# A transformer layer on one core: the second feed-forward product as seven products of block sums

## The chip, the core and the metric

The kernel runs on one core of a Trainium2 chip. The core has a matrix engine (TensorE, "PE" in the profile, with its weight loads as "PEld"), a vector engine (VectorE, "DVE"), a scalar engine (ScalarE, "ACT"), GpSimd ("POOL", hardly used here) and a queue that issues the transfers (SyncE, "SP"). Matrix results go to eight PSUM banks of 128 x 512 fp32; operands lie in SBUF.

The metric is the time of one execution on the device in microseconds (us). Before the change it is 2343.2 us, the median of 3 runs (2342.2 to 2344.59).

## What is computed

One layer for 512 tokens of width 2048, all in fp32: a modulated norm, two mixers, an output projection, a second modulated norm and a gated feed-forward part. The change concerns the last lines:

```python
h = rms_norm(x, norm2_g[layer]) * (1.0 + sc2) + sh2
gate, up = jnp.split(h @ w_ffn_in[layer], 2, axis=-1)
x = x + g2 * ((jax.nn.silu(gate) * up) @ w_ffn_out[layer])
```

The hidden width is 5632, that is 44 tiles of 128. The product with `w_ffn_in` is called the first product here, that with `w_ffn_out` the second.

## The kernel before

**Layout.** Activations lie feature by feature: a tile has 128 features on the partitions and the tokens (T = 512) along the free axis. Output feature tile m (16 of them) is thus a 128 x 512 matrix.

**Precision.** An fp32 matrix product is made of three fast ones. `split` (L208) makes of a weight tile a rounded high part (ScalarE, L212) and the rest (VectorE, L213). `three` (L219) multiplies high by high, high by low and low by high into one accumulator. The pools `hi` and `lo` have three buffers each, so `split` can run two tiles ahead of the one in use. Splits have a raised priority (`AHEAD`), by which the program that orders each engine's queue places them earlier than their place in the code.

**First product (L1015 to L1047).** For each f from 2 to 43 it is already made by seven products for eight: weights and activations are cut into blocks (two halves of k, gate and up for the weights; two token halves, HT = 256, for the activations), sums of blocks are made on VectorE (L1022 to L1025), and `product` (L898) runs 24 matmuls of 256 columns for each of the seven. Results are taken from PSUM by `tap` (L993, ScalarE). At the end `keep` (L1000) multiplies the gate by up, splits the 512 columns into a high and a low part and writes both to DRAM (`actd`, 512 KB for each f). While f is below 18, one task of `rest` per f also makes one column of the modulation vector from a 128 x 2048 matrix (`ada`, L185, and `gemv`, L178, on VectorE).

**Second product (L1051 to L1087).** The 44 tiles of hidden features are taken in chunks of 8, 12, 12 and 12, since all of them don't fit into SBUF. For each chunk and each m the weights `w_fo[m]` are loaded and split, and for each hidden tile `three` multiplies: the weights are stationary, the 512 tokens move. The accumulated 128 x 512 result is multiplied by the gate column and added to `x2[m]` by one fused operation on VectorE (L1083), and after the last chunk written to the output (L1085). Activations of the next chunk come in meanwhile (`load_acts`, L1055). That is 44 x 16 x 3 = 2112 matmuls of 512 columns.

**Order.** Each engine has a queue of its own, executed in order; the order in it was worked out ahead of time from priorities and readiness. All loads and stores are on SyncE's queue.

## Time and profile before

| what | us |
|---|---|
| median of 3 runs | 2343.2 (2342.2 to 2344.59) |
| the profiled execution | 2343.62 |
| its span, first to last instruction | 2341.8 |
| all work ahead of f = 2 of the first product | 0 to 1009.76 |
| first product, f = 2 to 43 | 1009.76 to 1859.30 |
| second product | 1859.30 to 2338.10 |
| what follows the last matmul | 2338.10 to 2341.8 |

In the first of these stages TensorE is busy for 975.62 us. Matmuls are pipelined, so the duration of one matmul in a row (0.389 us for 512 columns) is longer than the distance from one to the next; times for TensorE are read from distances between starts, or from the length of a piece over its count. The same holds, in a smaller way, for VectorE.

### The profile page before, as it was taken

Reading aid. Unit: us, or ns where it says so; the run is one execution under the profiler, and the core shown is the slowest. Engines: PE = TensorE matmul, PEld = TensorE weight load, DVE = VectorE, ACT = ScalarE, POOL = GpSimd, SP = SyncE. Lnnn points to the kernel's source line nnn. Section 1 sums busy time; section 2 is a strip of 40 time slices with the busy share of each in tenths; the row PEclk is TensorE's granted clock in tenths of the full one; section 3 lists DMA queues with packets and bytes.
Section 4 is the critical chain, followed back from the end, with each engine's and each line's share of the span. In section 5 each row is a group of like instructions: output and inputs, shape, how many; then the busy total and the mean of one; then the engine's idle time right before and its main releaser. Section 6 shows DMA issues by size and latency. Waiting matters only on the chain.

```text
span 2341.8 us, 35224 instructions
## 1 busy us (share of the span) xinstructions
PE 2303.9 (98%) x14371; PEld 2106.8 (90%) x14371; DVE 1646.8 (70%) x2208; ACT 1027.8 (44%) x1833; POOL 10.7 (0%) x25
## 2 busy tenths in 40 slices
PE   8999899999999999989999999999999999999999
PEld 6899899888888788989999999999999988888887
DVE  8887778998887864898888877777777633333332
ACT  4325665566556422744444444444444321222221
POOL 0000000000000000000000000000000000000000
PEclk9999999999999999999999999999999999999999
DMA  9886446843322575335544433333333584253331
GB/s 371 314 309 220 168 148 246 300 155 108 111 106 73 186 285 185 131 140 189 184 177 174 168 127 135 136 135 136 135 136 123 209 324 146 95 202 95 105 136 61
DMA packets 77549, 402.99 MB, mean 172 GB/s; under 512 B 8622, under 2 KB 9292, under 8 KB 47564
## 3 DMA queue, kind: packets, MB, share of 16 engines
q1 hardware_dynamic: 77388, 400.75, 47.4%
q8 instruction: 112, 1.84, 0.3%
q14 instruction: 49, 0.40, 0.0%
HBM read 369.24 MB, written 31.47 MB: 171 GB/s over the span
## 4 chain that ended last, share of the span: by engine, by line
PE 90%; DVE 6%; ACT 2%; issue 1%; DMA 1%; SPq 0%; ACTq 0%; DVEq 0%
PE ffA L92 21%; PE fo L92 20%; PE ffC L92 10%; PE sbp L92 7%; PE wo L92 7%; PE ffB L92 5%; PE st L92 4%; PE hgf L92 4%; PE hgq L92 3%; PE hgg L92 3%; PE l L92 1%; PE sbo L92 1%; DVE ada L178 1%; PE hgo L92 1%; PE r L92 0%
## 5 line engine op out<-in xcount | busy, mean ns | idle before, releaser
L92 PE MATMUL fo<-act,wfo_0h 128*128 128x512 f32 x1024 | 315.2, 389 | 0.0
L178 DVE SCALAR_TENSOR_TENSOR ada<-ada,cond 128x2048 f32<-128x2048 f32 x95 | 216.5, 2284 | 37.1 <-DMA ada<-in_w_ada 37.1
L92 PEld LDWEIGHTS fo<-act,wfo_0h 128*128 128x128 f32 x1024 | 192.1, 188 | 39.9
L92 PE MATMUL fo<-act,wfo_0l 128*128 128x512 f32 x512 | 199.2, 389 | 0.0
L1083 DVE SCALAR_TENSOR_TENSOR x<-fo,mod,x 128x512 f32<-128x512 f32 x64 | 48.0, 751 | 133.4 <-PE fo L92 124.5
L92 PE MATMUL ffA<-opA,ff_1h 128*128 128x256 f32 x672 | 125.0, 286 | 6.3 <-ACT sg L1011 6.3
L92 PE MATMUL ffB<-opA,ff_2h 128*128 128x256 f32 x672 | 123.0, 283 | 0.0
L92 PE MATMUL ffA<-opB,ff_6h 128*128 128x256 f32 x672 | 122.8, 283 | 0.0
L92 PE MATMUL ffC<-opB,ff_7h 128*128 128x256 f32 x672 | 122.8, 283 | 0.0
L92 PE MATMUL ffA<-opC,ff_5h 128*128 128x256 f32 x672 | 122.8, 283 | 0.0
L92 PE MATMUL ffC<-opC,ff_4h 128*128 128x256 f32 x672 | 122.8, 283 | 0.0
L92 PE MATMUL ffA<-opD,ff_3h 128*128 128x256 f32 x672 | 122.8, 283 | 0.0
L92 PE MATMUL fo<-act,wfo_8h 128*128 128x512 f32 x384 | 118.2, 389 | 0.0
L92 PEld LDWEIGHTS fo<-act,wfo_0l 128*128 128x128 f32 x512 | 96.1, 188 | 19.9
L92 PEld LDWEIGHTS ffA<-opA,ff_1h 128*128 128x128 f32 x672 | 106.6, 195 | 6.5 <-ACT sg L1011 6.5
L92 PEld LDWEIGHTS ffB<-opA,ff_2h 128*128 128x128 f32 x672 | 105.1, 193 | 0.0
L92 PEld LDWEIGHTS ffA<-opB,ff_6h 128*128 128x128 f32 x672 | 104.8, 192 | 0.0
L92 PEld LDWEIGHTS ffC<-opB,ff_7h 128*128 128x128 f32 x672 | 104.8, 192 | 0.0
L92 PEld LDWEIGHTS ffA<-opC,ff_5h 128*128 128x128 f32 x672 | 104.8, 192 | 0.0
L92 PEld LDWEIGHTS ffC<-opC,ff_4h 128*128 128x128 f32 x672 | 104.8, 192 | 0.0
L92 PEld LDWEIGHTS ffA<-opD,ff_3h 128*128 128x128 f32 x672 | 104.8, 192 | 0.0
L92 PE MATMUL ffA<-opA,ff_1l 128*128 128x256 f32 x336 | 96.1, 286 | 0.0
(1553 smaller groups left out, 6452.8 us busy)
## 6 DMA issues: line engine op xcount, KB each, us to landing
ada<-in_w_ada SPq DMA_DIRECT2D x95, 1024.0 KB, 5.2
actd<-pair SPq DMA_DIRECT2D x44, 512.0 KB, 2.6
act<-actd SPq DMA_DIRECT2D x44, 512.0 KB, 6.4
fix<-in_w_fix SPq DMA_DIRECT2D x14, 1024.0 KB, 5.8
wsb_0r<-in_w_sb SPq DMA_DIRECT2D x8, 768.0 KB, 4.1
wsb_2r<-in_w_sb SPq DMA_DIRECT2D x8, 768.0 KB, 4.3
wsb_4r<-in_w_sb SPq DMA_DIRECT2D x8, 768.0 KB, 4.4
wsb_6r<-in_w_sb SPq DMA_DIRECT2D x8, 768.0 KB, 6.0
```

The lines of the kernel that those rows point to most:

```text
L92: self.engine.matmul(out, lhsT, rhs, **kw)
L178: V.scalar_tensor_tensor(w, w, 1.0, row, op0=ALU.mult, op1=ALU.mult, accum_out=col)
L1083: V.scalar_tensor_tensor(x2[m], out, mcol(G2, m), x2[m], op0=ALU.mult, op1=ALU.add)
```

## The change

The second product is made by seven products for eight as well. The hidden features are taken in pairs of tiles (22 pairs), the 2 x 2 blocks of the activations are two tiles of a pair by two token halves of 256, those of the weights two tiles of a pair by two halves of the 2048 output columns. Sums of activation blocks are made once, when the first product delivers them, and written to DRAM as seven operands with a high and a low part each; sums of weight blocks are made on VectorE ahead of their splits. The roles in the matmul turn round: 128 tokens of an operand are stationary, 512 output columns of weights move. So results come out with tokens on the partitions; they are collected in `O` (128 x 4 x 2048), and in the last chunk 64 transposes on TensorE turn them back, each pair followed by the fused operation and a store.

The chunks are now 4, 4, 4, 4, 3 and 3 pairs. A unit is a chunk and one of two groups of 512 columns in each column half; per unit seven products run over the chunk's pairs in the order 2, 1, 7, 6, 4, 5, 3. Product 2 accumulates in PSUM over all chunks (`B`); the others are copied out by ScalarE (`onto`) or added to `O` by VectorE.

In the first product, `keep` collects two f in one tile of eight blocks (`forms`), and five small tasks (`later`: two of sums, three of splitting and storing) run between the products of the next f. A fourth pair of split buffers serves every fourth split. `x1d` becomes one DRAM tensor.

```diff
-CHUNKS = (8, 12, 12, 12)
+CHUNKS = (4, 4, 4, 4, 3, 3)
+ORDER = (2, 1, 7, 6, 4, 5, 3)
...
+    spare, count = [], [0]
+
     def split(r, shape, name):
-        hi = wp.tile(shape, F32R, tag="hi", name=name + "h")
-        lo = wp.tile(shape, F32R, tag="lo", name=name + "l")
+        count[0] += 1
+        if spare and count[0] % 4 == 0:
+            hi, lo = spare[0](shape, name)
+        else:
+            hi = wp.tile(shape, F32R, tag="hi", name=name + "h")
+            lo = wp.tile(shape, F32R, tag="lo", name=name + "l")
...
     def tap(src, name):
         t = tp.tile([P, HT], F32, tag="tap", name=name, bufs=4)
-        S.copy(t, src)
+        with tc.high_priority(offset=2 * AHEAD):
+            S.copy(t, src)
         return t
...
+    def load_op(c, q):
+        if c < len(CHUNKS):
+            nc.sync.dma_start(place(7 * c + q)[:, 0:CHUNKS[c]].bitcast(F32),
+                              opd[c][:, ORDER[q] - 1].rearrange("p n (h t) -> p n h t", h=2))
+
+    def load_y(u, b):
...
+        t = raw_tile([P, n, T], f"wfo{u}_{b}") if b % 2 == 0 else yraw[u > 0][:, b // 2, 0:n]
+        nc.sync.dma_start(t, a["w_fo"][i, b][:, starts[c]:starts[c] + n])
+        blocks[u][b] = t
...
+    def begin_second():
+        places.append(fh.tile([P, 4, 4, 2, HT], F32R, tag="b1", name="opsA"))
+        load_op(0, 0)
+        load_y(0, 2)
+        load_op(0, 1)
+        load_y(0, 0)
+        yraw.append(hp.tile([P, 3, 4, T], F32, tag="hhi", name="yraw0"))
+        load_y(0, 1)
+        load_y(0, 3)
+        load_op(0, 2)
+        load_op(0, 3)
+        places.append(hp.tile([P, 4, 4, 2, HT], F32R, tag="hlo", name="opsB"))
+        for q in range(4, 7):
+            load_op(0, q)
...
     def keep(f, sg, up):
-        V.tensor_mul(sg, sg, up)
-        pair = tp.tile([P, 2, T], F32R, tag="pair", name=f"pair{f}")
-        S.copy(pair[:, 0], sg)
-        V.tensor_sub(pair[:, 1], sg, pair[:, 0].bitcast(F32))
-        nc.sync.dma_start(actd[f], pair.bitcast(F32))
...
+        if f % 2 == 0:
+            V.tensor_mul(R[:, 0:8:7], sgv, upv)
+            return
+        V.tensor_mul(R[:, 1:4:2], sgv, upv)
...
+        def sums(a):
+            if a == 0:
+                V.tensor_add(R[:, 4], R[:, 7], R[:, 3])
+                V.tensor_sub(R[:, 5], R[:, 4], R[:, 0])
+            else:
+                V.tensor_sub(R[:, 6], R[:, 0], R[:, 7])
+                V.tensor_sub(R[:, 2], R[:, 1], R[:, 5])
+
+        def parts(a, b):
+            q = slice(a, b)
+            if f < FM - 1:
+                hi = tp.tile([P, b - a, HT], F32R, tag="fhi", name=f"fhi{f}_{a}", bufs=1)
+            else:
+                hi = cond[:, a * HT:b * HT].rearrange("p (q t) -> p q t", q=b - a).bitcast(F32R)
+            S.copy(hi, R[:, q])
+            V.tensor_sub(R[:, q].bitcast(F32R), R[:, q], hi.bitcast(F32))
+            for i, t in enumerate((hi.bitcast(F32), R[:, q])):
+                nc.sync.dma_start(opd[c][:, q, n - starts[c], i * HT:i * HT + HT], t)
+
+        later.extend([partial(sums, 0), partial(sums, 1), partial(parts, 0, 3), partial(parts, 3, 5), partial(parts, 5, 7)])
...
+    def multiply(out, c, q, raw, first, u, sums):
+        n = CHUNKS[c]
+        x = place(7 * c + q)
+        for k0 in range(0, n, 2):
+            w = min(2, n - k0)
+            with tc.high_priority(offset=AHEAD):
+                for d, e, g in sums:
+                    V.tensor_sub(*(t[:, k0:k0 + w] for t in (d, e, g)))
+            whi, wlo = split(raw[:, k0:k0 + w], [P, w, T], f"wfo{u}_{q}_{k0}")
+            for j in range(2):
+                js = slice(j * P, j * P + P)
                 for kk in range(w):
...
+                    k = k0 + kk
+                    flags = dict(stop=False, skip_group_check=True)
+                    PE.matmul(out[j], x[:, k, 0, js], whi[:, kk], start=first and k == 0, **flags)
+                    PE.matmul(out[j], x[:, k, 0, js], wlo[:, kk], start=False, **flags)
+                    flags["stop"] = k == n - 1
+                    PE.matmul(out[j], x[:, k, 1, js], whi[:, kk], start=False, **flags)
...
+    def onto(dst, src, first):
+        if first:
...
+                S.copy(dst, src)
+            return
+        t = cond[:, taps[0] % 4 * T:taps[0] % 4 * T + T]
...
+            S.copy(t, src)
+        V.tensor_add(dst, dst, t)
...
+    def emit_out(m, th):
+        ps = slots[turn[0] % len(slots)]
...
+        for j in range(2):
+            PE.transpose(ps[:, j * P:j * P + P], src[:, j], ident2)
...
+        V.scalar_tensor_tensor(src, ps.rearrange("p (j t) -> p j t", j=2), mcol(G2, m),
+                               xr.rearrange("p (j t) -> p j t", j=2), op0=ALU.mult, op1=ALU.add)
+        nc.sync.dma_start(a["y"][m][:, th * HT:th * HT + HT].rearrange("p (j t) -> p j t", j=2), src)
...
+        for q, p in enumerate(ORDER):
+            out = {2: B[i], 7: C, 4: C}.get(p, A)
+            raw = {2: y[2], 1: y[0], 7: y[1], 6: t2, 4: y[2], 5: y[0], 3: y[3]}[p]
+            sums = {7: [(y[1], y[3], y[1])], 6: [(t2, y[3], y[0])], 4: [(y[2], y[2], t2)]}.get(p, ())
...
+            multiply(out, c, q, raw, p in (1, 7) or p == 2 and first, u, sums)
+            if final:
+                some_out(3)
...
+            if p == 1:
+                ready(0, 0)
+                if final:
+                    slots += [t[:, h * HT:h * HT + HT] for t in B[i] for h in range(2)]
...
+            if q < 4 and i == (c == 0):
+                load_op(c + 1, q)
+            if i == 1 and 1 <= q < 4:
+                load_op(c + 1, q + 3)
+    some_out(len(outs))
```

## The prediction

> **What bounds the kernel now.** I read the page from the top: span, engines, granted clock.

> ```profile
> span 2341.8 us, 35224 instructions
> ...
> PE 2303.9 (98%) x14371; PEld 2106.8 (90%) x14371; DVE 1646.8 (70%) x2208; ACT 1027.8 (44%) x1833; POOL 10.7 (0%) x25
> ...
> PEclk9999999999999999999999999999999999999999
> ```

> TensorE is busy nearly all the time at nearly full clock, so only less work for it can help much. Next the chain that ended last, in order of time: the last two first-product pieces, then the second product.

> ```profile
> 1816.12 5.76 PE ffA L92 x48
> 1836.28 5.76 PE ffA L92 x48
> 1859.32 478.76 PE fo L92 x2112
> ```

> The second product is one unbroken piece of 2112 matmuls: 478.76 / 2112 = 0.2267 us each. No other engine appears in it. In the first product the same piece returns every 20.16 us, one column tile f. Then the stages: first product while vectors of `ada` are still being made, first product after that, second product.

> ```profile
> core 0: us, PE busy (x) PEld busy (x) DVE busy (x) ACT busy (x) POOL busy (x), PEclk, DMA share, GB/s
> 1009.76:1346.00 336.24, 336.24 (x2780) 336.24 (x2781) 287.84 (x308) 160.88 (x236) 0.00 (x0) 0.99 0.49 179
> 1346.00:1859.30 513.30, 513.30 (x4279) 513.30 (x4278) 382.65 (x404) 242.19 (x355) 0.00 (x0) 1.00 0.37 136
> 1859.30:2338.10 478.80, 478.76 (x2113) 396.07 (x2111) 157.54 (x175) 96.38 (x112) 0.00 (x0) 1.00 0.44 152
> ```

> TensorE has no gap in any of them. VectorE (DVE) is at 86%, 75% and 33%. The change takes work from TensorE and gives it to VectorE, so the question is how near VectorE comes to the new bound.

> **The matmuls.** Per block of k the new form runs 7 products x 2 token blocks x 3 terms; over 22 blocks and 2 column halves that is 22 x 2 x 42 = 1848 matmuls, all 512 wide, for 2112. Their roles turn round: activations stationary, weights moving. The stage `st` already runs so:

> ```profile
> 59.83 0.39 PE L92 MATMUL st<-wi8h,hhi 128*128 128x512 f32 x1
> ...
> 63.91 0.39 PE L92 MATMUL st<-wi9h,hlo 128*128 128x512 f32 x1
> ```

> These two of its rows stand 18 matmuls apart: 4.08 / 18 = 0.2267 us, the same pitch. So 264 x 0.2267 = **-59.9 us**, and the new product lasts 1848 x 0.2267 = 418.9 us.

> **The transposes.** 16 column tiles x 2 token halves x 2 = 64 are new. The kernel has such transposes, four at a time between matmuls:

> ```profile
> 264.05 0.60 PE L97 MATMUL otpsb<-cst,orowsb 128*128 128x128 f32 x4
> 264.41 0.42 PE L92 MATMUL sbp<-wsb_1l,hhi 128*128 128x384 f32 x1
> ```

> ```profile
> L97 PE MATMUL otpsb<-cst,orowsb x32: 270/272/273, 264.1 to 485.1; 128*128 128x128 f32 x32
> ```

> Four hold the queue for 0.36 us, 0.09 each. By the order of the emits 46 to 52 lie ahead of the last matmul: **+4.5 us**, bounds 4 and, were each to take its own 0.27 us, 14. [...]

> **VectorE's prices.** From the timeline, and from the line view for ScalarE:

> ```profile
> 1014.15 0.69 DVE L1001 TENSOR_TENSOR sg<-sg,up 128x512 f32<-128x512 f32 x1
> 1014.76 1.22 DVE L1025 TENSOR_TENSOR wg2r<-wg2r 128x1024 f32<-128x1024 f32 x1
> ```

> ```profile
> 1003.51 4.45 DVE L875 TENSOR_TENSOR opC<-x,opC 128x256 fp32r<-128x256 f32 x13
> ```

> ```profile
> 1413.99 1.21 DVE L213 TENSOR_TENSOR ff_2l<-wg22r,ff_2h 128x1024 fp32r<-128x1024 f32 x1
> 1415.12 1.21 DVE L1022 TENSOR_TENSOR ffS<-wu23r 128x1024 f32<-128x1024 f32 x1
> ```

> ```profile
> L212 ACT CAST ff_5h<-ffS 128x1024 fp32r<-128x1024 f32 x17 | 17.8, 1047 | 10.2 <-PE ffB L92 10.2
> L1003 ACT CAST pair<-sg 128x512 fp32r<-128x512 f32 x18 | 11.2, 620 | 5.0 <-DVE sg L1001 5.0
> ```

> Back to back VectorE spends 1.13 us on 1024 columns, 0.61 on 512, 0.34 on 256 (4.45 / 13). ScalarE's cast is 1.05 and 0.62 us.

> **First product.** Per pair of f the old `keep` had two subtractions of 512 columns (1.22). The new one has four sums of 256 (1.36) and three subtractions of 768, 512 and 512 (0.87 between the prices above, 0.61, 0.61): 3.45. That is +2.2 per pair, +1.1 per f. ScalarE gains less and is at half. The products' matmuls stay. After 1346 us VectorE goes to (382.65 + 25.5 x 1.1) / 513.3 = 80%: hidden. Before it, with the `ada` vectors, it goes to (287.84 + 16.7 x 1.1) / 336.24 = 91%, unevenly, since all five tasks of a pair run in the even f:

> ```profile
> L178 DVE SCALAR_TENSOR_TENSOR ada<-ada,cond x16: 2280/2282/2289, 1007.9 to 1314.3; 128x2048 f32<-128x2048 f32 x16
> ```

> An even f has 11 x 1.13 (splits and weight sums) + 3 x 0.34 + 0.61 + 3.45 + 2.28 = 19.8 us of VectorE in TensorE's 20.16; an odd one 16.3. VectorE executes in order and waits for casts:

> ```profile
> DVE ff_1l L213 <- ACT ff_1h L212: 23.4, 15, 1.6
> DVE ff_3l L213 <- ACT ff_3h L212: 18.6, 14, 1.5
> ```

> These 42 us are 2.6 per f. If they stayed, an even f would need 22.4, an odd one 18.9, so 41.3 in 40.3: 1 us lost per pair, some 8 pairs, 8 us. But the waits end at a buffer that TensorE frees, and the change adds a further pair of split buffers to every fourth split; VectorE can then run further ahead. Bounds 0 and +9 us; I take **+2**, nearer the waits that cost TensorE nothing now.

> The added DMA issues (six per pair for two) wait on SyncE's queue for VectorE, and weight loads of a later f stand behind them. Those loads are due about a whole f before use now (the row of 1415.12 sums weights of f=23 while f=22 is running), so a delay of a few us is covered; without this cover each would show whole. The single `fhi` buffer makes ScalarE's cast wait for the transfer of the part before it, with weight casts queued behind; the further split buffers cover one such wait of some 3 us. Both are inside the bounds above.

> **The hand-over.** Operands and weights of the first block come in from the moment product 2 of the last f ends, 5 x 2.88 = 14.4 us ahead of the end of the first product (48 matmuls, two products, take 5.76). The DMA rates by slice, 2.5 us each from 1860:

> ```profile
> GB/s 233 282 374 406 415 401 401 401 407 404 403 406 408 400 401 404 265 135 141 174 84 382 99 351 378 294 395 279 408 237 355 0 0 160 170 344 357 199 238 7
> ```

> At about 400 GB/s 1 MB takes 2.6 us. Product 2 needs two, and the four issued first land in 10.4 us, ahead of the end. The seventh and eighth (product 7's and 6's operands) land about 21 us after the first issue, 6.6 us into the stage; they are wanted at 10.9 and 16.3 (24 x 2 x 0.2267 = 10.9). Bounds 0 and +6 (a load that stands behind the last pair's writes); I take **+1**.

> **Second product, VectorE.** A unit with 4 blocks has 14 split and 8 weight-sum subtractions of 1024 columns and, after the first block, 12 additions of 512: 22 x 1.13 + 12 x 0.61 = 32.2 us against TensorE's 168 x 0.2267 = 38.1. A unit with 3: 11 x (1.13 + 0.61) + 7.3 = 26.5 against 28.6, 93%. The last two add two additions and about ten of the final fused operations each (0.40, from the row below less the 0.08 overlap that the 1.21 rows show): 31.7 against 28.6 + 1.8 for transposes. So the last two units overrun by 1.3 us each, which the split buffers partly absorb. ScalarE (14 casts and 8 copies per unit) is at about half. Loads: 15 MB per 4-block chunk in 76 us, 200 GB/s, half of the rate above. Bounds 0 and +12; I take **+2**.

> **The end.** Now the last matmul is followed by one fused operation and one transfer:

> ```profile
> 2337.68 0.39 PE L92 MATMUL fo<-act,wfo_8l 128*128 128x512 f32 x1
> 2338.10 0.75 DVE L1083 SCALAR_TENSOR_TENSOR x<-fo,mod,x 128x512 f32<-128x512 f32 x1 [7.41 <-PE fo L92]
> 2338.88 0.33 SPq L1085 DMA_DIRECT2D out_y<-x  x1
> ```

> ```profile
> L920 DVE SCALAR_TENSOR_TENSOR x<-wo15h,mod,xr x2: 475/480/484, 948.7 to 956.8; 128x256 f32<-128x256 f32 x2
> ```

> From 2338.07 to 2341.8 is 3.7 us. Afterwards follow two additions (1.2), transposes, 6 to 9 fused operations of 256 columns (2.4 to 3.6) and a transfer (2.9): 7 to 8.3. So **+4**, bounds +3 and +5.

> **The sum**, on the profiled execution (2343.62 us, span 2341.8 and 1.8 around it; the median 2343.2 is 0.4 below and I keep the working unshifted): 2343.6 - 59.9 + 4.5 + 2 + 1 + 2 + 4 = **2297 us**. With the low ends 2343.6 - 59.9 + 4 + 3 = 2291, with the high ends of all but the transposes 2320.

> **The rivals.**

> A: VectorE is uncovered in part: the `ada` turns lose their 9 us and the three-block units their 12, perhaps the hand-over too. For it speak the 98% of an even f and the 93%; against it that TensorE now sees none of the waits. 2343.6 - 59.9 + 4.5 + 9 + 4 + 12 + 4 = about 2317, between 2306 and 2335. Chance 0.20.

> B: each pair of transposes writes one half of a bank whose other half VectorE still reads. If the second pair waits for that read, TensorE loses 0.27 + 0.48 and up to 1.1 of VectorE's queue, 16 times: 12 to 30 us, 2309 to 2327. Against it: the four transposes above are followed at once by other matmuls, as a queue that is ordered by readiness would do here. Chance 0.07. [...]

> C, slower than before: VectorE stands behind its cast at every split of the second product. Before, it does at the short splits:

> ```profile
> DVE wfo_8l L213 <- ACT wfo_8h L212: 177.9, 47, 3.8
> ```

> There the wait is free, with VectorE at 33%. Now VectorE has 8 x 32.2 + 2 x 26.5 + 2 x 31.7, less 10 additions in each of the first two units (12 us), some 362 us of work. Waiting out 140 casts of 1.05 and 28 of 0.62 adds 164: 526 us, 47 more than the 479 of now, and with the end and the first product some 2397 us. It decides from about 110 us of such waits, two casts in three. Against it: a cast needs only a freed buffer, and TensorE spends 12 x 0.2267 = 2.7 us on each 1024-column piece with two more split. Chance 0.06.

> D: the saving is nearly eaten (waits between A and C), within 0.2% of the time before. Chance 0.04. That the matmuls are not cheaper by count I hold excluded by the rows; a longer pitch from moving weights is in A.

> **How the numbers follow.** The forecast, 2288 to 2305, has 0.63. Faster by over 0.2% (about what a measurement of this kernel can tell from no change) is forecast, A and B: 0.90. Within: 0.04. Slower: 0.06. The range reaches over B and most of A, up to 2325; below, 2288 leaves 3 us for waits that the sum counts and that do not come.

> **What would show it.** Matmuls of the second product 0.227 us apart, 1848 of them, in about 425 us with transposes: right. Idle TensorE before L92 with VectorE's `lo` as releaser, in the even f before 1346 us or in the last four units: A. TensorE idle ahead of L97, released by the fused operation: B. A second product over 480 us with VectorE waiting for casts: C. Idle at about 1859 us with DMA as releaser: the hand-over was mis-sized.

## The result, and the profile after

| | before | after |
|---|---|---|
| median | 2342.7 us (4 runs, 2341.57 to 2344.59) | 2312.17 us (4 runs, 2309.45 to 2315.23) |
| ratio | | 0.9869, 95% interval 0.9852 to 0.9886 |
| profiled execution, its span | 2343.62, 2341.8 | 2309.45, 2307.6 |
| ahead of the first product | 1009.8 | 1008.2 |
| first product | 849.5 | 842.3 |
| second product, to its last matmul | 478.8 | 448.8 |
| behind the last matmul | 3.7 | 8.3 |

The change saves 30.5 us, or 1.3%; on the two profiled executions it is 34.2. The forecast was 46.3 on the profiled execution. The time lies 15 us above the point: above the band of 2288 to 2305 us, to which the prediction gave a chance of 0.63, and inside the range, which reaches to 2325.

The page of the changed kernel, as before from the top:

```profile
span 2307.6 us, 35720 instructions
...
PE 2253.1 (98%) x14171; PEld 2049.8 (89%) x14171; DVE 1919.5 (83%) x2570; ACT 1160.1 (50%) x2011; POOL 10.7 (0%) x25
```

TensorE's share of the span is what it was, with 50.8 us less of busy time. That 98% hides what is new: waits of 0.2 to 3.4 us, each too short to show in a slice of 58 us. The stages show where they are (columns as in the same view of before):

```profile
1008.20:1346.00 337.80, 335.33 (x2803) 334.68 (x2804) 310.16 (x352) 167.22 (x246) 0.00 (x0) 0.99 0.55 196
1346.00:1850.50 504.50, 504.06 (x4256) 503.65 (x4256) 412.48 (x466) 252.29 (x368) 0.00 (x0) 1.00 0.46 161
1850.50:2299.30 448.80, 436.20 (x1896) 349.70 (x1896) 374.21 (x422) 211.90 (x269) 0.00 (x0) 1.00 0.56 198
```

VectorE stands at 92, 82 and 83%; the forecast had 91 and 80 for the first two, and 362 us of work in the third, where 374 were measured. So its amount was forecast well, and TensorE is idle 12.6 us in the third stage all the same. TensorE's waits between 1000 and 2310 us, the largest of them, by who ended them (total us, times, longest):

```profile
PE ffA L93 <- ACT sg L1104: 6.2, 1, 6.2
PE foA L93 <- ACT O L1196: 3.4, 1, 3.4
PE foC L93 <- DVE wfo_2l L221: 2.7, 5, 0.5
PE ffA L93 <- ACT u L1008: 2.2, 2, 1.4
PE foB L98 <- DVE O L1213: 2.0, 2, 1.0
PE foC L93 <- DVE opsB L221: 1.9, 2, 1.2
```

The first stands ahead of f = 2 and was there before the change (6.3 us). The others are new. They hold the causes, not the full price: matmuls are pipelined (one of 512 columns takes 0.39 us, and the next starts 0.227 us after it), so starts fall behind by more than the idle time shown. In the tables below, "lost" is worked out from the starts in the second product, the transposes of the end with it: wherever two lie over 0.3 us apart, what exceeds 0.227 us. In the changed kernel that is 25.8 us, about 22 of them unforeseen.

### The profile page after: what moved, and what is told of

Its sections match the earlier page's. It is cut to its first block, busy times and chain, and to the rows that moved or that the text cites. A ratio compares the mean times of both kernels' runs of the same rounds, so it can differ in the third digit from the quotient of the medians.

```text
span 2307.6 us, 35720 instructions
## 1 busy us (share of the span) xinstructions
PE 2253.1 (98%) x14171; PEld 2049.8 (89%) x14171; DVE 1919.5 (83%) x2570; ACT 1160.1 (50%) x2011; POOL 10.7 (0%) x25
## 4 chain that ended last, share of the span: by engine, by line
PE 79%; DVE 11%; DMA 4%; ACT 3%; issue 3%; SPq 0%; DVEq 0%; ACTq 0%
PE ffA L93 17%; PE ffC L93 9%; PE foA L93 8%; PE sbp L93 8%; PE wo L93 7%; PE ffB L93 4%; PE foC L93 4%; PE st L93 4%; PE hgf L93 4%; PE hgq L93 3%; PE hgg L93 3%; PE foB L93 1%; DVE ada L180 1%; PE l L93 1%; DMA opd<-fhi 1%
## 5 line engine op out<-in xcount | busy, mean ns | idle before, releaser
L93 PE MATMUL ffA<-opD,ff_3h 128*128 128x256 f32 x512 | 93.6, 283 | 0.8 <-ACT u L1008 0.8
L93 PE MATMUL ffA<-opB,ff_6h 128*128 128x256 f32 x512 | 93.6, 283 | 0.2 <-ACT a L1008 0.2
L93 PE MATMUL ffC<-opB,ff_7h 128*128 128x256 f32 x512 | 93.5, 283 | 0.0
L93 PE MATMUL ffC<-opC,ff_4h 128*128 128x256 f32 x496 | 90.8, 284 | 0.4 <-ACT c L1008 0.3
L93 PE MATMUL ffB<-opA,ff_2h 128*128 128x256 f32 x496 | 91.3, 284 | 0.0
L93 PE MATMUL ffA<-opC,ff_5h 128*128 128x256 f32 x496 | 90.6, 283 | 0.0
L93 PE MATMUL ffA<-opA,ff_1h 128*128 128x256 f32 x496 | 90.6, 283 | 0.0
L1082 ACT CAST fhi<-forms 128x512 fp32r<-128x512 f32 (+1 forms) x63 | 43.6, 692 | 90.6 <-DMA opd<-fhi 74.1
L93 PEld LDWEIGHTS ffA<-opD,ff_3h 128*128 128x128 f32 x512 | 79.8, 192 | 1.0 <-ACT u L1008 1.0
L93 PEld LDWEIGHTS ffA<-opB,ff_6h 128*128 128x128 f32 x512 | 79.7, 192 | 0.4 <-ACT a L1008 0.4
L93 PEld LDWEIGHTS ffC<-opB,ff_7h 128*128 128x128 f32 x512 | 79.8, 192 | 0.0
L93 PEld LDWEIGHTS ffC<-opC,ff_4h 128*128 128x128 f32 x496 | 77.2, 192 | 0.8 <-ACT c L1008 0.8
L93 PEld LDWEIGHTS ffB<-opA,ff_2h 128*128 128x128 f32 x496 | 77.7, 193 | 0.1
L93 PEld LDWEIGHTS ffA<-opC,ff_5h 128*128 128x128 f32 x496 | 77.3, 192 | 0.0
L93 PEld LDWEIGHTS ffA<-opA,ff_1h 128*128 128x128 f32 x496 | 77.3, 192 | 0.0
L1083 DVE TENSOR_TENSOR forms<-forms,fhi 128x512 fp32r<-128x512 f32 (+1 forms) x63 | 49.0, 778 | 31.0 <-ACT fhi L1082 30.6
L93 PE MATMUL ffA<-opD,ff_3l 128*128 128x256 f32 x256 | 72.5, 283 | 0.0
L93 PE MATMUL ffC<-opB,ff_7l 128*128 128x256 f32 x256 | 72.4, 283 | 0.0
L93 PE MATMUL ffA<-opB,ff_6l 128*128 128x256 f32 x256 | 72.4, 283 | 0.0
L93 PE MATMUL ffB<-opA,ff_2l 128*128 128x256 f32 x248 | 70.3, 284 | 0.0
L93 PE MATMUL ffA<-opA,ff_1l 128*128 128x256 f32 x248 | 70.2, 283 | 0.0
```

The lines of the kernel that those rows point to most:

```text
L93: self.engine.matmul(out, lhsT, rhs, **kw)
L1082: S.copy(hi, R[:, q])
L1083: V.tensor_sub(R[:, q].bitcast(F32R), R[:, q], hi.bitcast(F32))
```

## The experiments

All edits start from the changed kernel; ratios are against the kernel before, which ran beside each and came to medians of 2342.78 to 2343.15 us. Each median is of 4 executions, that of no_weight_sums of 2. "First" runs from the first matmul of f = 2 to the first of the second product, "second" from there to the end of the last transpose, both in the profiled execution.

| run | median us (lowest to highest) | ratio, 95% | first | second | lost |
|---|---|---|---|---|---|
| changed kernel | 2312.17 (2309.45 to 2315.23) | 0.9852 to 0.9886 | 842.1 | 453.1 | 25.8 |
| no_weight_sums | 2289.4 (2288.52 to 2290.28) | 0.9753 to 0.9792 | 842.9 | 431.3 | 4.8 |
| order100 | 2297.47 (2294.3 to 2299.11) | 0.9791 to 0.982 | 845.3 | 440.6 | 13.8 |
| gpsimd_sums | 2354.25 (2351.13 to 2359.05) | 1.0036 to 1.0066 | 841.8 | 496.7 | 69.3 |
| early_keep | 2306.12 (2303.21 to 2308.97) | 0.9829 to 0.9859 | 843.5 | 447.9 | 20.5 |
| order_and_keep | 2294.62 (2291.16 to 2298.42) | 0.9781 to 0.981 | 840.9 | 438.0 | 11.2 |
| order0_and_keep | 2297.63 (2294.7 to 2299.28) | 0.9787 to 0.982 | 843.7 | 439.0 | 12.0 |
| no_fourth | 2326.28 (2324.49 to 2328.48) | 0.9916 to 0.9945 | 848.6 | 461.4 | 34.2 |
| pad192 | 2321.15 (2317.39 to 2321.84) | 0.9886 to 0.9919 | 852.6 | 453.0 | 25.8 |
| pad224 | 2316.06 (2314.51 to 2319.3) | 0.9873 to 0.9903 | 850.8 | 453.9 | 26.7 |
| shift64 | 2321.34 (2317.48 to 2324.1) | 0.9893 to 0.9923 | 841.9 | 458.9 | 23.4 |
| shift192 | 2324.38 (2320.58 to 2329.08) | 0.99 to 0.9933 | 846.4 | 455.7 | 24.3 |
| shift256 | 2309.77 (2304.86 to 2314.76) | 0.9833 to 0.9876 | 845.3 | 453.1 | 25.7 |

One execution of a kernel differs from the next by 2 to 10 us here, so a difference of a stage in one profile below some 3 us decides nothing by itself.

### VectorE's sums in the second product

The theory: in a unit VectorE has time enough on average, but its queue holds sums that nobody needs yet ahead of a split that TensorE is waiting for. The rows that led to it are VectorE's timeline of the changed kernel around product 7 of a four-block unit, and below it TensorE's:

```profile
1975.93 1.22 DVE L221 TENSOR_TENSOR opsB<-yraw,opsB 128x1024 fp32r<-128x1024 f32 x1
1977.07 1.22 DVE L1181 TENSOR_TENSOR yraw<-yraw 128x1024 f32<-128x1024 f32 x1
1978.20 1.22 DVE L1181 TENSOR_TENSOR T<-yraw,wfo 128x1024 f32<-128x1024 f32 x1
1979.34 1.22 DVE L1181 TENSOR_TENSOR wfo<-wfo,T 128x1024 f32<-128x1024 f32 x1
1980.48 1.22 DVE L221 TENSOR_TENSOR wfo_2l<-yraw,wfo_2h 128x1024 fp32r<-128x1024 f32 x1
```

```profile
1980.83 0.39 PE L93 MATMUL foC<-wfo_2h,opsC 128*128 128x512 f32 x1
1981.75 0.50 PE L93 MATMUL foC<-wfo_2l,opsC 128*128 128x512 f32 x1 [0.53 <-DVE wfo_2l L221]
```

At 1980.83 TensorE multiplies by the high part of product 7's second piece and needs the low part 0.23 us later. VectorE starts on it at 1980.48, because from 1978.20 it made `T` and `wfo`, the weights of products 6 and 4: neither is due before product 7 is over. Had one of the two sums come later, there would be no wait. As it is, the next start comes 0.92 us after the last instead of 0.23.

**no_weight_sums** leaves out all sums of weight blocks in the second product:

```diff
-            raw = {2: y[2], 1: y[0], 7: y[1], 6: t2, 4: y[2], 5: y[0], 3: y[3]}[p]
-            sums = {7: [(y[1], y[3], y[1])], 6: [(t2, y[3], y[0])], 4: [(y[2], y[2], t2)]}.get(p, ())
-            if p == 7:
...
-                        V.tensor_sub(y[0][:, ks], y[1][:, ks], y[0][:, ks])
+            raw = {2: y[2], 1: y[0], 7: y[1], 6: y[3], 4: y[2], 5: y[0], 3: y[3]}[p]
+            sums = ()
```

> The second product without any of its sums of weight blocks (products 7, 6, 4 and 5 take unsummed blocks, so the result is another), all matmuls, splits, additions, loads and transposes kept. Theory 'VectorE's weight sums': the gaps of TensorE from 1976 us on, some 19 of the 24.6 us, go; only the one at 1867 to 1874 us stays: second product 428 to 434 us for 448.8, time 2291 to 2298 us. Rival 'split buffers' (a cast waits for TensorE to free a buffer whatever VectorE does): gaps at products 7, 6 and 4 stay, second product over 442 us, time 2303 us or more.

The second product is 21.8 us shorter, and what is lost in it falls from 25.8 to 4.8 us. So nearly all of it hangs on these sums; the time is 1.6 us below the range expected. It doesn't yet tell their amount from their place in the queue.

**order100** keeps every sum and lowers the priority of those for products 6 and 4:

```diff
-            with tc.high_priority(offset=AHEAD):
+            with tc.high_priority(offset=AHEAD if q == 2 else 100):
                 for d, e, g in sums:
```

> The weight sums of products 6 and 4 keep a smaller raised priority (100 for 300), so that in VectorE's queue the low part of product 7's second piece stands ahead of product 4's sums, and the additions to O are spread; all work is kept. Theory 'order of VectorE's queue' (the sums stand ahead of a split that TensorE waits for): the gaps of 0.7 us at product 7's second piece and their 0.1 us followers go, and part of the 1.4 us ones of the three-block units: 4 to 9 us of the 19, 2302 to 2308 us. Rival 'amount' (VectorE has more to do in that stretch than TensorE, in whatever order): the gaps move to product 6 or 4 and the sum stays, 2308 to 2316 us.

VectorE's timeline of this kernel, same unit:

```profile
1977.80 1.22 DVE L1181 TENSOR_TENSOR T<-yraw,wfo 128x1024 f32<-128x1024 f32 x1
1978.94 0.68 DVE L1266 TENSOR_TENSOR O<-foA,O 128x512 f32<-128x512 f32 x1
1979.54 1.21 DVE L221 TENSOR_TENSOR wfo_2l<-yraw,wfo_2h 128x1024 fp32r<-128x1024 f32 x1
1980.67 2.35 DVE L1181 TENSOR_TENSOR wfo<-wfo,T 128x1024 f32<-128x1024 f32 x2
```

The split now starts 0.94 us earlier, ahead of the sums of `wfo`, and no wait is left in the four-block units. The median is 14.7 us lower with the same work on VectorE (1918.0 us busy against 1919.5): it is the place in the queue, not the amount, that cost these. The gain is above what was expected because the hand-over (below) gains too: of the 12.0 us less that are lost, 7.2 are in the four-block units, 2.2 in the last two units, and 2.6 at the hand-over, where the wait falls from 3.43 to 2.40 us. What stays are the three-block units: some 10 of the 12 us lost there before the last matmul. The chain of waits of order100 there:

```profile
2225.95 0.69 DVE wfo L1245
2226.64 1.74 DVE yraw L1181 x2
2228.37 1.14 DVE T L1181
2229.51 1.15 DVE wfo_0l L221
2230.65 0.04 issue
2230.70 2.34 PE foC L93 x9
```

Five operations of VectorE end on a matmul of product 7. Four of them are sums; only `T` could still go behind the split.

**gpsimd_sums** gives the sums of products 6 and 4 to GpSimd, which is idle otherwise:

```diff
-                    V.tensor_sub(*(t[:, k0:k0 + w] for t in (d, e, g)))
+                    (V if q == 2 else G).tensor_sub(*(t[:, k0:k0 + w] for t in (d, e, g)))
```

> The weight sums of products 6 and 4 (8 of 22 operations of 1024 columns per four-block unit) go to GpSimd, which has nothing to do here. Theory 'amount': VectorE is relieved of 9 us per unit and the gaps of the second product mostly go, second product 430 to 438 us for 448.8, time 2295 to 2303 us. Rival 'GpSimd is too slow or holds up VectorE': if one of its operations lasts over about 4 us, products 6 and 4 wait for it, and the time is over 2316 us.

The edit moves 4 of the 22 operations of a four-block unit, not the 8 that the expectation counts. The kernel is slower than the one before. The timelines of GpSimd and, below, of VectorE in this kernel show one reason:

```profile
2026.13 3.31 POOL L1181 TENSOR_TENSOR T<-yraw,wfo 128x1024 f32<-128x1024 f32 x1 [29.59 <-DVE wfo L1245]
2029.52 3.23 POOL L1181 TENSOR_TENSOR wfo<-wfo,T 128x1024 f32<-128x1024 f32 x1
```

```profile
2025.92 1.22 DVE L221 TENSOR_TENSOR wfo_2l<-wfo,wfo_2h 128x1024 fp32r<-128x1024 f32 x1
2027.06 3.47 DVE L1181 TENSOR_TENSOR yraw<-yraw 128x1024 f32<-128x1024 f32 x1
2030.45 3.39 DVE L1245 TENSOR_TENSOR wfo<-yraw,wfo 128x1024 f32<-128x1024 f32 x1
```

Without GpSimd beside it, a VectorE operation of 1024 columns takes 1.22 us; with it 3.4, about as long as GpSimd's own. By the ends it isn't slowed but waits its turn: the first ends at 2030.53, 1.09 us after GpSimd's `T` (2029.44), the second at 2033.84, 1.09 us after GpSimd's `wfo` (2032.75), and all 35 lengthened operations of 1024 columns from 1900 us on end 1.08 to 1.09 us after one of GpSimd's. An addition that takes one operand from PSUM isn't lengthened (here beside a sum of GpSimd from 2241.38 to 2244.20):

```profile
2241.89 0.68 DVE L1266 TENSOR_TENSOR O<-foA,O 128x512 f32<-128x512 f32 x1
```

So 48 sums on GpSimd took nothing off VectorE: its busy time in the whole kernel rose from 1919.5 to 1958.5 us, though it had 48 operations less. A second part of the price is the clock's: the granted clock in the second product is 0.95 here and 1.00 in the changed kernel, and 5% of 492 us is 25 us, the most that it can explain of the 43.5 us more that are lost.

### The hand-over

The longest wait that the change brought stands where the second product begins. The chain of waits of the changed kernel shows it step by step:

```profile
1861.40 5.45 PE foC L93 x24
1866.86 0.03 ACTq L220
1866.88 0.04 issue
1866.92 1.04 ACT wfo_2h L220
1867.97 1.77 ACT cond L1082 x3
1869.74 0.49 ACT O L1196
1870.23 0.04 issue
1870.27 7.36 PE foA L93 x24
```

Product 6 needs the bank of product 1, which ScalarE has to copy into `O` first. Product 1 was over at 1861.4. But ahead of the copy in ScalarE's queue stand a weight cast, which can't start before TensorE leaves a split buffer at 1866.9, and three casts of the last pair of f (`parts`). No transfer is in the chain. Afterwards the first 24 matmuls take 7.36 us instead of 5.44.

**early_keep** gives the last pair's steps a higher priority, so that they come ahead of the second product's casts:

```diff
-        V.tensor_mul(R[:, 1:4:2], sgv, upv)
+        with tc.high_priority(offset=2 * AHEAD if f == FM - 1 else 0): V.tensor_mul(R[:, 1:4:2], sgv, upv)
...
     while later:
-        one_later()
+        with tc.high_priority(offset=2 * AHEAD): one_later()
```

> The last pair's product, sums, casts and stores (f = 42 and 43) get raised priority, so that they stand ahead of weight sums in the queues and ScalarE's copies of product 1 into O no longer stand behind them and behind casts that wait for TensorE. Theory 'order at the hand-over': the gap of 3.6 us at 1866.7 us and the half clock after it (1.8 us) go, time 5 us lower, 2304 to 2309 us. Rival 'O waits for the old tiles' stores' (the copy's own wait on a transfer): the copy is as late as before, no change, 2309 to 2316 us. A little may be lost again where the moved 4 us of VectorE work delay the splits of products 7 and 6.

ScalarE's timeline of this kernel has the copy behind no cast of the last pair (those start at 1856.83, 1858.30 and 1859.77):

```profile
1865.33 1.05 ACT L220 CAST wfo_2h<-yraw 128x1024 fp32r<-128x1024 f32 x1
1866.28 1.07 ACT L1196 COPY O<-foA 128x512 f32<-128x512 f32 x2
```

The wait is gone, what is lost falls by 5.3 us and the median by 6.0.

**order_and_keep** makes both edits at once. **order0_and_keep** does too, with priority 0 in place of 100, so that the sums come as late as their place in the code.

> order100 and early_keep together. Theory: the two mend different gaps (four-block units at product 7, and the hand-over), so the gains of 14.7 and 6.0 us add up to 2288 to 2295 us. Rival: the hand-over's gap was partly mended by order100 already (it fell from 3.6 to 2.6 us there), and the gains overlap: 2294 to 2299 us.

> The same with the sums of products 6 and 4 at no raised priority at all. Theory 'order': additions and low parts stand ahead of still more sums, the three-block units lose their gaps of 1.4 us too: 2283 to 2291 us. Rival 'amount': in the three-block units VectorE has 26.5 us of work for TensorE's 28.6, and what goes first only moves the gap, to products 6 and 4, whose sums are now late: 2291 to 2300 us.

The two gains add up to 17.6 us, 3.1 less than 14.7 + 6.0, because order100 had already won 2.6 us at the hand-over: there they overlap, as the rival said, and the time lies where the two expectations meet. At 2294.62 us, ratio 0.9795 (0.9781 to 0.981), order_and_keep is the fastest complete kernel of this study. With priority 0 nothing more is won. The waits at product 7 shrink, and others come at the end of the stage (1.7 us once for a cast, 2.4 for the fused operations): the time lies in the rival's range. That VectorE's work has no slack left to be moved in there fits the prediction's count (26.5 us of it to 28.6, in the last two units 31.7 to 30.4), but no run separates this from a better order.

### The first product: matmuls of 113 and of 120 ns

The first product should have become 2 us longer and is 7.2 shorter. In the changed kernel's chain of waits two of the pieces of 48 matmuls last

```profile
1210.45 5.76 PE ffA L93 x48
1230.45 5.60 PE ffA L93 x48
```

In the second, 24 of the 48 read their weights from the fourth pair of split buffers. Worked out from all starts: 5279 matmuls with weights in the usual buffers lie 120 ns apart, the 1776 with weights in the fourth pair 113 to 114. That is 1776 x 6.7 ns = 11.8 us.

**no_fourth** takes that pair out of the first product:

```diff
-    spare.append(spare_here)
...
-    spare[0] = spare_there
+    spare.append(spare_there)
```

> The changed kernel with the fourth pair of split buffers taken out of the first product alone (all its splits use the three usual pairs, as before the change); the second product keeps it. Theory 'place': the quarter of the matmuls that came at 113.3 ns comes at 120 again, 1776 x 6.7 ns = 11.9 us, and VectorE can run one split less ahead, so that the first product's gaps grow from 4.3 us by 0 to 8: first product 854 to 862 us for 842.1, time 2323 to 2333 us. Rival 'the fourth buffer gained by hiding waits': the pitch by operand stays as it is, and only gaps grow.

All 7055 matmuls are now 120 ns apart. The first product takes 848.6 us, and the view of waits lists none of TensorE's in it: VectorE's added work is hidden there with three buffers too. So the fourth pair did its good by the pitch, and not by letting VectorE run ahead. The rest of this run's loss isn't the pitch. The hand-over's wait is 12 us (timelines of TensorE and, below, of ScalarE; L1195 of this kernel is L1196 above):

```profile
1885.70 4.48 PE L93 MATMUL foA<-opsB,opsA 128*128 128x512 f32 x12 [12.00 <-ACT O L1195]
```

```profile
1885.06 1.07 ACT L1195 COPY O<-foA 128x512 f32<-128x512 f32 x2 [7.26 <-DMA opd<-forms]
```

So here the copy into `O` waits for a transfer, the store of the last pair. That store is late because VectorE comes to the last pair's product only at 1873.85, behind sums and splits of the second product. Why the copy needs that store to be over in this kernel and not in the changed one is not shown.

Why does a buffer make a matmul faster? The first theory was the low bits of the weights' own address, the rival the region of SBUF. **pad192** and **pad224** put a tile of 192 or 224 bytes into the first pool at the left end of SBUF: the usual split buffers and the activations behind it move alike, the fourth pair (in a pool at the right end) stays. The edit of the first:

```diff
-    cond = const.tile([P, D], F32, name="cond")
+    pad, cond = const.tile([P, 48], F32, name="pad"), const.tile([P, D], F32, name="cond")
```

> All left-side tiles of the changed kernel move up by 192 bytes (a padding tile ahead of the first); the right-side ones stay. In the profile of the changed kernel the 256-column matmuls of the first product stand 120.0 ns apart with weights in the usual split buffers (start address 288 modulo 512) and 113.3 with weights in the fourth pair (480 modulo 512, right side). Theory 'low address bits of the stationary tile': with 480 modulo 512 everywhere on the left, all products come at 113.3 ns (the first product 42 x 126 x 6.7 ns = 35 us shorter), and every other matmul with its stationary operand on the left loses 6.7 ns too, 1848 of them in the second product = 12 us; in all 50 to 80 us, 2230 to 2262 us. Rival 'region': only the right side is fast; no change, 2308 to 2316 us.

> As before with 224 bytes, so that left-side tiles start at 0 modulo 512. Theory 'low address bits': a row of 512 bytes no longer crosses a 512-byte boundary; as fast as with 192 bytes or faster, 2215 to 2262 us. Rival 'region': no change, 2308 to 2316 us. If 192 is fast and 224 is not, the bits that decide are those by which 32 and 96 modulo 128 differ.

Both theories fell. The usual buffers, which moved, keep 120 ns; the fourth pair, which didn't, goes to 120 (pad192) and 117 (pad224). What had changed for it was its distance from the activations, and from the other tiles that moved with them. **shift64**, **shift192** and **shift256** put the tile between the usual split buffers and the activations, so that the activations move, with all that lies behind them, and the weights do not. The edit of the first (48 and 64 in the others):

```diff
     wp = ctx.enter_context(tc.tile_pool(name="wp", bufs=3))
+    ctx.enter_context(tc.tile_pool(name="gp", bufs=1)).tile([P, 16], F32, name="pad")
```

> In the two padded runs the weights in the fourth split buffers came at 120 ns too as soon as the activations' tiles had the same start address modulo 256 as those buffers (224 and 224), and at 113.3 when the two differed by 192 (after: 224 against 32). So theory 'same low bits': the matrix engine reads the next weights while the activations stream, and the two reads hold each other up when their addresses agree modulo 256. Here 64 bytes lie between the split buffers and all later left-side tiles: usual buffers at 32, activations at 96 (difference 192, as in the fast case), fourth buffers at 224 (difference 128). Theory: first product at 113.3 ns in the usual buffers, 25 to 35 us shorter; the other stages and the second product lose 6.7 ns per matmul where weights and activations lie so and TensorE is the bound; in all 40 to 80 us, 2230 to 2270 us. Rival 'region' (only weights at high addresses are fast, and the padded runs slowed them for another reason): 120 ns stay, 2306 to 2318 us.

> The same with 192 bytes: usual split buffers at 32, activations at 224 (difference 64), fourth buffers at 224 (difference 0). Theory 'same low bits': usual buffers 113.3 ns, the fourth ones 120, so some 12 us less gained in the first product than with 64 bytes, or as much if the sign of the difference matters; 2240 to 2285 us. Rival 'region': no change, 2306 to 2318 us.

> A tile of 256 bytes between the pool of the usual split buffers and the activations, in place of the 64 and 192 bytes tried before. Theory 1 (what counts of the place repeats after 256 bytes): the matmuls are as in the changed kernel, 113.3 ns apart where the weights are in the fourth pair of split buffers and 120 in the usual ones, 227 at 512 columns in the second product, and the time is 2309 to 2315 us. Theory 2 (what counts is the region or the distance itself, or a longer period): 116 to 120 ns in both, perhaps 229 to 233 at 512 columns, and 2316 to 2325 us.

Median distance from one matmul to the next, by how far the activations moved against the weights (from the starts):

| moved by, bytes | usual buffers, 256 columns | fourth pair, 256 columns | second product, 512 columns |
|---|---|---|---|
| 0 | 120 ns | 113 | 227 |
| 64 | 118 | 119 | 233 |
| 192 | 118 | 120 (shift192 and pad192) | 230 |
| 224 | not tried | 117 | not tried |
| 256 | 120 | 113 | 227 |

So what counts in the first product is how the weights lie to the activations, or to a tile that moves with them, and it is the same again after 256 bytes: shift256 moves the same tiles as shift64 and shift192 and gives back all three values. The theory of shift64, 113 ns in the usual buffers, fell. In the second product there is more to it: there the fourth pair lies inside a tile of activations (`opsB`), so that its weights move with them, and still its matmuls go from 227.5 ns on average to 229.2 (shift64) and 230.3 (shift192; distances below 260 ns). In one kernel the two sets of buffers answer in opposite ways, so a shift that helps one part costs another: shift64 wins some 10 us on the usual buffers (5279 x 2 ns) and loses as much on the fourth pair (1776 x 5.7), 6 in the second product, and 7 ahead of the first (it begins at 1015.4 us, not 1008.2). Of these 7, 2.6 come between 768 and 780 us, where the granted clock is 0.66 for 10 us (1.00 in the changed kernel), the rest in part from the pitch of the 512-wide products there (231 ns for 227 in `hgf`, 229 in `wo`). Which distances are good, and why, these runs do not settle.

## Why the prediction was right, and where it was wrong

**Right.** The matmuls: 1848 of them 227 ns apart, the -59.9 us. The transposes: one takes 0.27 us by its row, and four between matmuls still 0.36 to 0.42 of TensorE's time. The end: 3.7 to 8.3 us, +4.6 for +4. No wait of TensorE is put down to a load. Rival C, waits for casts at every split, did not come. Rival B came twice in the last unit, 2.0 us in all in the row `foB L98 <- DVE O L1213`, and not 16 times. Rival A had the right sign, TensorE idle with VectorE's low part as releaser, and in part the right place: the three-block units lost some 12 us, which is its price. Its `ada` turns cost TensorE at most one wait of 1.4 us, and the four-block units were not in it. The measured 2312.17 us lies in A's range (2306 to 2335, chance 0.20) and not in the forecast's.

**Wrong, term by term**, on the profiled execution: forecast 2343.6 - 46.3, measured 2343.6 - 34.2.

- *"Bounds 0 and +12; I take +2"* for VectorE in the second product: some 19 us (25.8 lost, less 3.6 + 1.7 at the hand-over and about 1 behind the last matmul); without the sums it is near nothing. 12 of them stand in the three-block units, where the point was taken near the low bound and the high bound came true. The other 7 stand in five of the eight four-block units, 1.4 to 1.5 each. The step that failed there is the sum over a unit, 32.2 us of VectorE against 38.1 of TensorE, taken as a sign that the unit is covered. The four sums of each half of a unit gather around product 7, and VectorE executes in order (in the rows of its timeline above the split of 1980.48 starts 1.14 us after the sum of 1979.34, and that 1.14 us after the sum of 1978.20), so the 6 us of slack lie elsewhere in the unit. The high bound failed for the same reason: it charged the three-block units alone. By order100, some 9 of the 19 go with a new order and no less work. The other 10, in the three-block units, fall to 2 without the sums; neither order that was tried wins them back.
- *"Bounds 0 and +6; I take +1"* for the hand-over: 5.3 us, inside the bounds but for another reason. The argument counted the landing of eight loads, and those were in time. It left out ScalarE's queue, on which casts that wait for buffers stand ahead of a copy that frees a bank. early_keep shows it.
- *"I take +2"* for the first product: -7.2. VectorE's +1.1 us per f was hidden fully (no_fourth has no wait). The gain, 11.8 us, came from a pitch that no row of before could show. It is partly given back: some 4 us of waits for ScalarE's `tap` copies, such as `ffA L93 <- ACT u L1008` above. The view of waits lists four. In the largest (1.43 us at 1150.57) the chain names an `ada` operation of VectorE. It puts two of the others behind a store: ScalarE's cast of a part can't start before the part ahead of it has left the single `fhi` buffer, and the copy that TensorE needs stands behind that cast. In the changed kernel:

```profile
1103.09 4.93 DMA opd<-fhi
...
1108.10 0.62 ACT fhi L1082
1108.72 0.28 ACT u L1008
```

```profile
ACT fhi L1082 <- DMA opd<-fhi: 74.1, 40, 3.8
```

The prediction had named this wait and held it for covered by the further split buffers. It came out the other way: without the fourth pair (no_fourth) the cast waits 24.7 us in 18 times, and TensorE not at all. Why is not shown.

The misses have different signs: +17 and +4.3 against -9, with -1.5 ahead of the first product, which neither kernel's edits explain and which is within what executions differ by. The forecast came nearer than its terms did, and that is luck: two terms that were too low met a gain that nobody foresaw. With all weights at 120 ns the change gives what pad192 measured, 2321.15 us, and not 2312.

## What to carry to other kernels

A share of busy time over a unit, even 84%, doesn't show that an engine which executes in order is hidden: write down for each item when it is due, and what stands ahead of it in its queue. Give work that is needed later a lower priority than a split that is needed now; here that was one number, worth 14.7 us. It helped where a unit had slack left (84% busy) and hardly where it had none (93% and more). Where a stage ends and another begins, look at each queue for items that wait for a buffer ahead of items that free one.

## What the runs showed of the hardware

The changed kernel, order100, gpsimd_sums and shift256:

```profile
1870.27 4.61 PE L93 MATMUL foA<-opsB,opsA 128*128 128x512 f32 x12 [3.43 <-ACT O L1196]
```

```profile
1871.47 3.03 PE L93 MATMUL foA<-opsB,opsA 128*128 128x512 f32 x12 [2.40 <-ACT O L1196]
```

```profile
2209.38 1.65 PE L93 MATMUL foA<-opsB,opsC 128*128 128x512 f32 x6 [3.32 <-DVE O L1266]
```

```profile
1150.43 0.65 PE L93 MATMUL ffA<-opD,ff_3hi 128*128 128x256 f32 x2 [1.79 <-ACT u L1008]
```

```profile
1150.60:1154.00 3.40, 3.40 (x17) 3.40 (x18) 3.25 (x4) 2.21 (x3) 0.00 (x0) 0.50 0.90 306
```
